# Padded on-chip pools and earlier first weight pieces in a two-layer hybrid trunk on one Trainium2 core

## The chip, the cores and the metric

The kernel runs on one core of one Trainium2 chip. The metric is the time of one execution on the device in microseconds; lower is better. Five engines of the core matter here: TensorE (PE) multiplies matrices, VectorE (DVE) and ScalarE (ACT) work element by element, GpSimd (POOL) does little, and SyncE (SP) issues nearly all DMA transfers. Each engine works through its own queue in order; semaphores make an engine wait for the result of another. SBUF is the on-chip memory that holds all operands, PSUM the one that receives products.

## The reference

Two layers, each a mixer and an MLP, on a residual stream of 512 tokens by 1024 features, all in float32:

```python
def rms_norm(x, gain):
    return x * rsqrt(mean(x * x, axis=-1) + 1e-6) * gain

# layer 0: mixer = multi-head latent attention (MLA), 8 heads
# layer 1: mixer = gated linear attention (GLA), 4 heads, chunks of 64
for i in range(2):
    xn = rms_norm(x, norm_mix[i])
    x = x + mixer_i(xn)                       # ends in "... @ w_o", 1024 x 1024
    xn = rms_norm(x, norm_mlp[i])
    hid = square(relu(xn @ w_up[i]))          # 1024 -> 4096
    x = x + hid @ w_down[i]                   # 4096 -> 1024
return rms_norm(x, final_norm)
```

GLA begins with `h = xn @ w_in`, whose columns are queries (512), keys (512), values (1024), gates (1024) and a low-rank forget gate (16). So the order of stages is: MLA, its output projection, MLP 0, GLA, its output projection, MLP 1, final norm.

## The kernel before

**Products.** Features lie on the 128 partitions, tokens along the rows: the stream is eight tiles `xT` of 128 by 512. To get float32 accuracy each operand is split into a rounded high part and a low part, and each product is three matmuls that add into one PSUM bank (`mm3`):

```python
    PE.matmul(psum, wh, xh, start=start, stop=False, **kw)   # L108
    PE.matmul(psum, wh, xl, start=False, stop=False, **kw)   # L109
    PE.matmul(psum, wl, xh, start=False, stop=stop, **kw)    # L110
```

A weight comes by DMA as `raw` or `wraw` and is split by `piece`: ACT rounds it into `wh` (L100), DVE subtracts into `wl` (L103); there are three buffers of each. So ACT and DVE make the weights that PE eats, one piece of 128 by 1024 for 24 matmuls of 256 columns or 12 to 24 of other widths.

**Output projection.** `out_proj` has four steps, c = 0 to 3. Each loads and splits 256 weight columns, multiplies two tiles (24 matmuls of 512 columns each), adds them to `xT` (DVE, L771), and hands each tile to the next norm: `add` starts the tile's square and its split into `x0h`, `x0l` to `x7h`, `x7l`, and `pair` builds the token-half combinations `T0` to `T3`.

**MLP.** The up product goes in blocks of 512 hidden columns; each block is cut in halves both ways, and seven products of quarters replace eight (steps `s1` to `s7`; "a11", "a12", "a21", "a22" are quarters of the weight, "11", "21", "22", "T1" to "T4" the combinations of x that meet them). The down product is arranged the same way. The last two blocks of the down product are plain: `down` makes eight tiles of 512 columns, adds them to `xT` (L1008) and hands them to the next norm, whose `add` is an ACT rounding (`set`, L232), an ACT square (`mt`), a DVE subtraction (`set`, L233) and a DVE sum (`acc`, L225).

**Where an MLP starts.** `mlp` is called after `out_proj`. It closes the pools `ps` and `stage`, opens `mps`, `down` and `down_w`, issues one 512-column matmul on the norm's last tile (`nrm.any`, L1056), and begins block 0 with `s1` (`unit`, a DMA of 512 KB; `piece`; 24 matmuls). Then `begin` finishes the norm: a mean over partitions by matmul (L242), then the reciprocal root on ACT and DVE (L119, L205 to L208).

**What sets the order.** The program is written without an order between engines; a scheduler puts each engine's instructions into its queue, by due time as it sees it, and buffers that come free. Pools are placed one after the other in SBUF, so the size of one sets the addresses of the next. The stationary operand of a matmul is the first after `psum` in the lines above, the moving one the second.

Of the kernel before, what the change touches and what calls it, by code (L numbers as in the profile page):

```python
# [18 lines left out]
P = 128  # L19
D = 1024  # L20
S = 512
# [28 lines left out]
def trunk_kernel(ctx: ExitStack, tc: tile.TileContext, t_in: dict, out: bass.AP, out_row: bass.AP):  # L50
# [93 lines left out]
    rk = rope_es.enter_context(tc.tile_pool(name="rope_keep", bufs=1, reuse_waits="tile"))  # L144
    gains = const.tile([P, N_GAIN], F32, name="gains")
    pos_i = rk.tile([P, NT], I32, name="pos_i")
    invf = rk.tile([P, 32], F32, name="invf")


# [98 lines left out]
    class QuadNorm(Norm):  # L248
# [7 lines left out]
        def scaled(self, j, src):  # L256
            pool = pool_of("up")
            lead = j < KH
            n = TH if lead else S
            hi, lo = (pool.tile([P, n], F32R, tag=f"x{j}{x}", name=uname(f"x{j}{x}")) for x in "hl")  # L260
            g = gcol(self.g, self.g0 + j)
            ACT.activation(hi, src[:, :n], AF.Copy, scale=g)
            DVE.scalar_tensor_tensor(lo, src[:, :n], g, f(hi), ALU.mult, ALU.subtract)
            if lead:
                self.quad["11"][j] = hi, lo
            else:
                self.any = hi
                for name, tk in (("21", first), ("22", second)):
                    self.quad[name][j - KH] = cut((hi, lo), slice(None), tk)

        def pair(self, k):
            pool = pool_of("up")
            g1, g2 = (gcol(self.g, self.g0 + j) for j in (k, k + KH))
            u, v = xT[k], xT[k + KH]
            t = pool.tile([P, 4, TH], F32, tag="raw", bufs=5, name=uname("pair"))
            t1, t2, t3, t4 = (t[:, i] for i in range(4))
            ACT.activation(t3, u[:, second], AF.Copy, scale=g1)
            DVE.scalar_tensor_tensor(t3, v[:, second], g2, t3, ALU.mult, ALU.subtract)
            DVE.scalar_tensor_tensor(t2, u[:, first], g1, t3, ALU.mult, ALU.add)
            DVE.scalar_tensor_tensor(t4, v[:, first], g2, t2, ALU.mult, ALU.subtract)  # L280
# [109 lines left out]
    def mla(layer, nrm, first, pools):  # L390
# [87 lines left out]
        for t in range(NT):  # L478
            tk = slice(t * P, (t + 1) * P)
            for hf in range(2):  # L480
                p = bank("bc"[hf])
                for k in range(2):
                    mm3(p, cut(CVL[k], slice(None), tk), cut(wv[k], slice(None), 0, slice(hf * 512, hf * 512 + 512)), k == 0, k == 1)
                if t == 0 and hf == 1:
                    pr = bank("b")
                    for i in range(NT):
                        tr(pr[:, i * 3 * RB : (i + 1) * 3 * RB], rows[:, i * P : (i + 1) * P])
                    cols = keep.tile([P, NT, 3], F32, tag="cols", name="cols")
# [267 lines left out]
        mms(range(n))  # L756
        return ps_, lambda: mms(range(n, ND))

    def out_proj(w2d, X, nxt, begun=None):
        for c in range(4):  # L760
            if c == 0:
                ps_, rest = begun or out_start(w2d, X, 0)
                rest()
            else:
                w = out_cols(w2d, c)
                ps_ = [bank("ac"[c % 2]), bank("ac"[c % 2])]
                for j in range(2):
                    a_type(ps_[j], w[j], X)
# [7 lines left out]
    def mlp(layer, nrm, nxt, final=False):  # L776
        w_up, w_dn = t_in["mlp_w_up"][layer], t_in["mlp_w_down"][layer]
        quad = nrm.quad
        NB = FF // FB
        closed("ps")  # L780
        opened("mps", space=bass.MemoryType.PSUM)
        closed("stage")
        dp, up, mp = opened("down"), pool_of("up"), pool_of("mps")
        wp = opened("down_w")

        def wide_raw():
            return wp.tile([P, 4, 512], F32, tag="raw", bufs=3, name=uname("raw"))

        def matmuls(p, w, k0, ks, ms, x, begin, end):
            for k in ks:  # L790
# [11 lines left out]

        def up_block(b):
            fh, s = b % 2, b // 2
            q = [dp.tile([P, 4, TH], F32, tag="q", bufs=6, name=uname("q")) for _ in range(2)]
            Q[s, fh] = q

            def unit(half, trail):
                if b == 1 and half == 0:
# [9 lines left out]
                return t  # L819

            def product(p, a, name, begin):
                w = piece(a, KH, 256)
                for j in range(2):
                    matmuls(p, w, 0, range(KH), [j], quad[name], begin, True)

# [7 lines left out]
                return t.rearrange("p (j t) -> p j t", j=2)  # L833

            def mt():
                return dp.tile([P, 512], F32, tag="mt", bufs=4, name=uname("mt"))

            v = {}

            def s1():  # L840
                a = v["a11"] = unit(0, 0)
                if b != 1:
                    v["a21"], v["a22"] = unit(1, 0), unit(1, 1)
                v["x1"] = bank("u")
# [5 lines left out]
                    seed(v["x1"])  # L850

            def seed(src):
                v["b2"] = mp.tile([P, 512], F32, tag="seed", name=uname("ps"))
# [46 lines left out]
            return [s1, s2, s5, s6, s3, s7, s4] if b < 2 else [s1, s5, s2, s6, s3, s7, s4]  # L900

        acc = {n: dp.tile([P, 4, TH], F32, tag=f"sum{n}", name=f"sum{n}_{layer}") for n in (1, 6, 7)}
        for n, (m0, tk) in {2: (0, first), 3: (0, second), 4: (KH, first), 5: (KH, second)}.items():
            acc[n] = xall[:, m0 : m0 + KH, tk]

        def down_block(s):
            last = s == NB // 2 - 2
# [78 lines left out]
            return [p1, p5, p6, p7, p2, p3, p4]  # L986

        def hidden(b, pool):
            hi, lo = (pool.tile([P, 4, S], F32R, tag="h" if pool is dp else "h" + x, bufs=2 if pool is dp else 1, name=uname("h" + x)) for x in "hl")
# [60 lines left out]
        def begin():  # L1050
            nrm.finish()
            for k in range(KH):
                DVE.tensor_tensor(xT[k][:, second], xT[k][:, second], xT[k + KH][:, second], ALU.subtract)

        t = mp.tile([P, 512], F32, tag="seed", name=uname("ps"))
        PE.matmul(t, nrm.any[:, :P], nrm.any, start=True, stop=True)  # L1056
# [19 lines left out]
        opened("ps", space=bass.MemoryType.PSUM)  # L1076
        hid = hidden(NB - 2, hp)
        down(NB - 2, hid)
        hid = hidden(NB - 1, dp)
        if final:  # L1080
            down_final(NB - 1, hid)
        else:
# [404 lines left out]
        opened("up", "right")  # L1487
        return QuadNorm(ND, inv_d, "mlp", g0, None)

    n_mlp0 = mlp_norm(0)  # L1490
    out_proj(t_in["mla_w_o"][0], O, n_mlp0, begun)

    class Mixer(Norm):
        def open(self):
            pool = opened("masks", "right")
            self.ident_i = pool.tile([P, P], I32, name="ident_i")
            DVE.tensor_copy(self.ident_i, ident)
            self.masks = {}
            for m in (1, 2, 4, 8):
# [9 lines left out]
    mlp(0, n_mlp0, n_mix1)  # L1509
    opened("stage")  # L1510
    Y = gla(0, n_mix1, "B", "B")
    closed("masks")
    n_mlp1 = mlp_norm(ND)
    out_proj(t_in["gla_w_o"][0], Y, n_mlp1)

    class Final:
        def open(self):
# [65 lines left out]
    mlp(1, n_mlp1, Final(), True)  # L1583
    for name in ("fin", "wide", "ps"):
        closed(name)


# [49 lines left out]
```

## Time and profile before

| | |
|---|---|
| median of 3 runs | 1122.13 us (1121.31 to 1123.38) |
| the profiled execution | 1124.27 us, of which the span is 1122.6 us |
| granted TensorE clock, mean | 0.983 |
| instructions | 17825 |
| MLA with its output projection | 0 to 196 us |
| MLP 0 | 196 to 532 us |
| GLA with its output projection | 532 to 777 us |
| MLP 1 and final norm | 777 to 1122.6 us |

Times inside the execution are counted from the start of the span. Where a row of the timeline reads "start us, us, engine line op out<-in", the second number is the instruction's own duration; consecutive matmuls overlap, so that the distance of two starts is what one costs. A number in square brackets at the end is how long the engine stood idle before that instruction, and what ended it. A row by windows gives, for each stretch, its length, then for PE, weight load, DVE, ACT and POOL the busy time with the count of instructions, then the granted clock and the share and rate of the DMA engines.

### The profile page before, as it was taken

Reading aid. Unit: us, or ns where it says so; the run is one execution under the profiler, and the core shown is the slowest. Engines: PE = TensorE matmul, PEld = TensorE weight load, DVE = VectorE, ACT = ScalarE, POOL = GpSimd, SP = SyncE. Lnnn points to the kernel's source line nnn. Section 1 sums busy time; section 2 is a strip of 40 time slices with the busy share of each in tenths; the row PEclk is TensorE's granted clock in tenths of the full one; section 3 lists DMA queues with packets and bytes.
Section 4 is the critical chain, followed back from the end, with each engine's and each line's share of the span. In section 5 each row is a group of like instructions: output and inputs, shape, how many; then the busy total and the mean of one; then the engine's idle time right before and its main releaser. Section 6 shows DMA issues by size and latency. Waiting matters only on the chain.

```text
span 1122.6 us, 17825 instructions
## 1 busy us (share of the span) xinstructions
PE 1087.1 (97%) x7320; PEld 994.2 (89%) x7320; DVE 892.7 (80%) x1210; ACT 641.0 (57%) x934; POOL 42.8 (4%) x78
## 2 busy tenths in 40 slices
PE   8999999889999999999799999999999999999997
PEld 6788887889999999987688888887989999999986
DVE  5789877889899899966365664667989899799865
ACT  5577654555666767653333743653556666776634
POOL 6300000000000000030000000000000000000000
PEclk9999999899999999999799999999999999999999
DMA  6412142133333423250232212431233523423312
GB/s 190 103 47 76 34 149 81 48 104 113 117 111 113 150 95 95 81 183 1 58 102 75 76 39 76 145 118 38 76 94 95 172 93 97 167 78 111 113 56 76
DMA packets 98001, 107.88 MB, mean 96 GB/s; under 512 B 8080, under 2 KB 72864, under 8 KB 97920
## 3 DMA queue, kind: packets, MB, share of 16 engines
q1 hardware_dynamic: 95904, 105.52, 29.9%
q10 hardware_dynamic: 1952, 1.21, 0.4%
q8 instruction: 57, 0.93, 0.3%
q0 software_dynamic: 64, 0.02, 0.1%
q14 instruction: 24, 0.20, 0.1%
HBM read 104.64 MB, written 2.10 MB: 95 GB/s over the span
## 4 chain that ended last, share of the span: by engine, by line
PE 87%; DVE 7%; ACT 2%; DMA 2%; issue 1%; SPq 0%; DVEq 0%; ACTq 0%
PE ps L108 27%; PE ps L110 27%; PE ps L109 26%; DVE wl L103 2%; PE ps L125 2%; PE ps L1301 2%; DMA wraw_ckv<-in_mla_w_in_dram 1%; ACT wh L100 1%; DMA raw<-in_mlp_w_up_dram 1%; DVE set L233 1%; DVE raw L877 1%; PE ps L656 0%; PE ps L1338 0%; PE ps L657 0%; PE ps L655 0%
## 5 line engine op out<-in xcount | busy, mean ns | idle before, releaser
L100 ACT ACTIVATE wh<-raw 128x1024 fp32r<-128x1024 f32 x208 | 219.8, 1059 | 183.4 <-PE ps L109 148.5
L103 DVE TENSOR_TENSOR wl<-raw,wh 128x1024 fp32r<-128x1024 f32 x208 | 252.6, 1224 | 22.5 <-ACT wh L100 21.8
L110 PE MATMUL ps<-h,wl 128*128 128x256 f32 x672 | 188.2, 280 | 2.8 <-DVE wl L103 2.7
L109 PE MATMUL ps<-h,wh 128*128 128x256 f32 x672 | 187.8, 280 | 0.0
L108 PE MATMUL ps<-h,wh 128*128 128x256 f32 x672 | 187.8, 279 | 0.0
L110 PEld LDWEIGHTS ps<-h,wl 128*128 128x128 f32 x672 | 126.4, 188 | 3.6 <-DVE wl L103 3.6
L109 PEld LDWEIGHTS ps<-h,wh 128*128 128x128 f32 x672 | 126.3, 188 | 0.0
L108 PEld LDWEIGHTS ps<-h,wh 128*128 128x128 f32 x672 | 126.3, 188 | 0.0
L108 PE MATMUL ps<-set,wh 128*128 128x512 f32 x232 | 93.5, 404 | 2.5 <-ACT set L232 2.5
L100 ACT ACTIVATE wh<-wraw 128x1024 fp32r<-128x1024 f32 x43 | 44.8, 1054 | 87.3 <-PE ps L110 42.4
L109 PE MATMUL ps<-set,wh 128*128 128x512 f32 x232 | 93.4, 403 | 1.0 <-DVE set L233 0.9
L110 PE MATMUL ps<-set,wl 128*128 128x512 f32 x232 | 92.8, 400 | 0.0
L103 DVE TENSOR_TENSOR wl<-wraw,wh 128x1024 fp32r<-128x1024 f32 x43 | 52.4, 1222 | 11.1 <-ACT wh L100 11.0
L103 DVE TENSOR_TENSOR h<-q,h 128x1024 fp32r<-128x1024 f32 x42 | 51.5, 1225 | 11.3 <-ACT h L100 11.3
L108 PE MATMUL ps<-wh,set 128*128 128x512 f32 x144 | 60.0, 417 | 0.0
L109 PE MATMUL ps<-wl,set 128*128 128x512 f32 x144 | 57.0, 396 | 0.0
L110 PE MATMUL ps<-wh,set 128*128 128x512 f32 x144 | 56.9, 395 | 0.0
L108 PEld LDWEIGHTS ps<-set,wh 128*128 128x128 f32 x232 | 44.5, 192 | 13.1 <-ACT set L232 3.1
L830 ACT ACTIVATE q<-q 128x512 f32<-128x512 f32 x64 | 40.0, 625 | 27.3 <-DVE q L829 26.9
L109 PEld LDWEIGHTS ps<-set,wh 128*128 128x128 f32 x232 | 44.5, 192 | 11.6 <-DVE set L233 1.7
L110 PEld LDWEIGHTS ps<-set,wl 128*128 128x128 f32 x232 | 44.6, 192 | 10.3
L100 ACT ACTIVATE h<-q 128x1024 fp32r<-128x1024 f32 x42 | 44.0, 1048 | 0.6 <-DVE q L964 0.6
(490 smaller groups left out, 3024.5 us busy)
## 6 DMA issues: line engine op xcount, KB each, us to landing
raw<-in_mlp_w_down_dram SPq DMA_DIRECT2D x38, 1024.0 KB, 5.3
raw<-in_mlp_w_up_dram SPq DMA_DIRECT2D x60, 512.0 KB, 3.8
wraw<-in_gla_w_in_dram SPq DMA_DIRECT2D x12, 1024.0 KB, 5.2
wraw<-in_mla_w_o_dram SPq DMA_DIRECT2D x8, 512.0 KB, 4.8
wraw<-in_gla_w_o_dram SPq DMA_DIRECT2D x8, 512.0 KB, 5.0
raw<-in_mlp_w_up_dram SPq DMA_DIRECT2D x2, 1024.0 KB, 6.6
xT<-in_x_dram SPq DMA_DIRECT2D x6, 256.0 KB, 8.3
wraw_qn<-in_mla_w_uq_dram SPq DMA_DIRECT2D x6, 256.0 KB, 3.4
```

Of the source, the lines that this page charges most:

```text
L100: order(ACT.activation(hi, src, AF.Copy))
L103: lo_eng.tensor_tensor(lo, src, f(hi), ALU.subtract)
L108: PE.matmul(psum, wh, xh, start=start, stop=False, **kw)
L109: PE.matmul(psum, wh, xl, start=False, stop=False, **kw)
L110: PE.matmul(psum, wl, xh, start=False, stop=stop, **kw)
L125: PE.transpose(psum, src, ident[: src.shape[0], : src.shape[0]])
L233: DVE.scalar_tensor_tensor(lo, src, g, f(hi), ALU.mult, ALU.subtract)
L830: ACT.activation(qs, qs, AF.Square)
L877: DVE.tensor_tensor(v["s"], v["s"], v["a11"], ALU.subtract)
L1301: PE.matmul(p[:, t * 64 : (t + 1) * 64].rearrange("p (n c) -> p n c", c=m), k[:, sl], later, start=True, stop=True)
```

## The change

**Pads.** Five pools get a dead first tile: `stage` 224 bytes per partition, a new pool `edge` on the right side 64, `up` 448, `masks` 256 and `rope_keep` 128 (`cols` moves into that pool). Read from the addresses of the two built programs: of 1664 matmuls with 512 columns, both operands now start at the same offset modulo 512 bytes, namely 416. Before, the pair (moving, stationary) was (480, 416) for 480 of them, (192, 416) for 480 and (416, 480) for 384; in the rest it was 0, 64 or 224 against 416, or 416 or 480 against 192. The 256-column matmuls stay as they were, nearly all at (480, 416) or (192, 416).

**First pieces of the MLPs.** `mlp` becomes a generator. `out_proj` runs it up to its first `yield` just after loading the weights of its last step, c = 3: a new step `s0` loads quarters a11 and a12 of block 0 and splits both. The pools are switched after that. Block 0 adds a21 + a22 in place and loads a22 once more for its last product (one more 512 KB transfer in each MLP). The matmul on `nrm.any` becomes two of 256 columns on `x0h`.

**First pieces of GLA.** In the last weight piece of MLP 0's `down`, `nxt.prefetch` loads the first 256 columns of GLA's `w_in` (1 MB) and splits two pieces into `self.qk`. No line of the program reads `self.qk`; `gla` loads and splits the same columns as before. The hidden tiles of MLP 0's last block move to the pool of those of the block before.

```diff
+    PADS = dict(stage=224, right=64, up=448, masks=256, keep=128)
+    def pad(pool, n):
+        if n:
+            pool.tile([P, n // 4], F32, tag="pad", name=uname("pad"))
...
-    opened("stage")
+    opened_stage()
+    pad(opened("edge", "right"), PADS["right"])
...
-    def out_proj(w2d, X, nxt, begun=None):
+    def out_proj(w2d, X, nxt, after, begun=None):
...
                 w = out_cols(w2d, c)
+                if c == 3:
+                    next(after)
...
-                w = piece(a, KH, 256)
+                w = v.pop(name) if name in v else piece(a, KH, 256)
...
+            def s0():
+                v["a11"], v["a12"] = unit(0, 0), unit(0, 1)
+                for name, a in (("11", v["a11"]), ("21", v["a12"])):
+                    v[name] = piece(a, KH, 256)
...
-                s = v["s"] = up.tile([P, KH, 256], F32, tag="raw", bufs=5, name=uname("raw"))
+                if b == 0:
+                    s = v["s"] = v["a22"]
+                else:
+                    s = v["s"] = up.tile([P, KH, 256], F32, tag="raw", bufs=5, name=uname("raw"))
...
             def s4():
+                if b == 0:
+                    v["a22"] = unit(1, 1)
...
+                    if b == NB - 1 and c == g == 1:
+                        nxt.prefetch(wide_raw())
...
-        PE.matmul(t, nrm.any[:, :P], nrm.any, start=True, stop=True)
-        blocks = [up_block(b) for b in range(NB)]
+        for h in range(2):
+            x = quad["11"][0][0]
+            PE.matmul(t[:, h * TH : (h + 1) * TH], x[:, :P], x, start=h == 0, stop=True, skip_group_check=True)
...
+        def prefetch(self, raw):
+            raw = raw.rearrange("p a (b n) -> p (a b) n", b=2)
+            SP.dma_start(raw, t_in["gla_w_in"][0][:, :256].rearrange("(k p) n -> p k n", p=P))
+            self.qk = [piece(raw[:, :, j * P : (j + 1) * P], ND, P) for j in range(2)]
```

Three places of the queues follow. Line numbers of the changed program are about ten higher in the helpers (L110 for L100, L113 for L103), and buffer numbers differ.

The first place is the end of MLA's output projection, on DVE, from the split of its last-but-one pair of tiles to the reciprocal root of the norm; `wl` rows are weight pieces. Before:

```order
L771 TENSOR_TENSOR xT<-ps_2136,xT 128x512
L278 SCALAR_TENSOR_TENSOR pair_2201<-xT,gains,pair_2201 128x256
L1053 TENSOR_TENSOR xT<-xT 128x256
L279 SCALAR_TENSOR_TENSOR pair_2201<-xT,gains,pair_2201 128x256
L103 TENSOR_TENSOR wl_2251<-raw_2243,wh_2250 128x1024
L263 SCALAR_TENSOR_TENSOR x7l_2195<-xT,gains,x7h_2194 128x512
L225 TENSOR_TENSOR acc_1930<-acc_1930,tmp_2198 128x512
L280 SCALAR_TENSOR_TENSOR pair_2201<-xT,gains,pair_2201 128x256
L281 SCALAR_TENSOR_TENSOR pair_2201<-xT,gains,pair_2201 128x256
L103 TENSOR_TENSOR T3l_2208<-pair_2201,T3h_2207 128x1024
L862 TENSOR_TENSOR raw_2391<-raw_2245,raw_2247 128x1024
L103 TENSOR_TENSOR wl_2299<-raw_2296,wh_2298 128x1024
```

After the change, from the last sum of a tile on:

```order
L274 SCALAR_TENSOR_TENSOR x7l_2213<-xT,gains,x7h_2212 128x512
L236 TENSOR_TENSOR acc_1936<-acc_1936,tmp_2216 128x512
L289 SCALAR_TENSOR_TENSOR raw_2219<-xT,gains,raw_2219 128x256
L884 TENSOR_TENSOR raw_2251<-raw_2249,raw_2251 128x1024
L290 SCALAR_TENSOR_TENSOR raw_2219<-xT,gains,raw_2219 128x256
L291 SCALAR_TENSOR_TENSOR raw_2219<-xT,gains,raw_2219 128x256
L912 TENSOR_TENSOR raw_2249<-raw_2141,raw_2249 128x1024
L113 TENSOR_TENSOR T3l_2226<-raw_2219,T3h_2225 128x1024
L216 SCALAR_TENSOR_TENSOR mt_2287<-ps_2280,mt_2285 128x512
L218 SCALAR_TENSOR_TENSOR mt_2289<-mt_2287,mt_2285 128x512
L113 TENSOR_TENSOR wl_2328<-raw_2324,wh_2327 128x1024
```

The two pieces of quarters a11 and a12 (`wl_2251`, `wl_2299` before) are gone from this stretch; they now stand ahead of the split of the last pair of tiles, and the first weight piece behind the last tile's sum is `wl_2328`, that of block 1.

The second place is ACT some 40 us further on, around the copies that seed the second block's products (L866 and L854 before, L888 and L873 after). Before:

```order
L100 ACTIVATE wh_2620<-raw_2328 128x1024
L100 ACTIVATE wh_2652<-raw_2549 128x1024
L830 ACTIVATE q_2227<-q_2227 128x512
L866 ACTIVATE mt_2584<-ps_2555 128x512
L854 ACTIVATE ps_2586<-mt_2359 128x512
```

After:

```order
L110 ACTIVATE wh_2617<-raw_2324 128x1024
L841 ACTIVATE q_2247<-q_2247 128x512
L888 ACTIVATE mt_2581<-ps_2552 128x512
L873 ACTIVATE ps_2583<-mt_2355 128x512
L110 ACTIVATE wh_2649<-raw_2546 128x1024
```

One rounding of a weight piece moved from ahead of the two copies to behind them.

The third place is the end of MLP 0, on DVE, in the last tiles of `down`; `raw_5768` is the load of `prefetch`:

```order
L236 TENSOR_TENSOR acc_5647<-acc_5647,mt_5692 128x512
L1035 TENSOR_TENSOR xT<-ps_5695,xT 128x512
L113 TENSOR_TENSOR wl_5771<-raw_5768,wh_5770 128x1024
L244 SCALAR_TENSOR_TENSOR set_5710<-xT,gains,set_5709 128x512
L236 TENSOR_TENSOR acc_5647<-acc_5647,mt_5713 128x512
L1035 TENSOR_TENSOR xT<-ps_5722,xT 128x512
L113 TENSOR_TENSOR wl_5775<-raw_5768,wh_5774 128x1024
L244 SCALAR_TENSOR_TENSOR set_5737<-xT,gains,set_5736 128x512
```

The two `wl` rows are new; before, the rows around them followed each other without them. On SP the new load stands ahead of GLA's own first load, which brings the same columns:

```order
L1021 DMA raw_5716<-in_mlp_w_down_dram 128x4x512
L1549 DMA raw_5768<-in_gla_w_in_dram 128x8x256
L140 DMA wraw_5830<-in_gla_w_in_dram 128x8x256
L140 DMA wraw_5906<-in_gla_w_in_dram 128x8x256
L140 DMA wraw_6058<-in_gla_w_in_dram 128x4x512
```

More of the change, by code (lines that the diff above doesn't have):

```diff
@@ L274, in pair @@
             u, v = xT[k], xT[k + KH]
-            t = pool.tile([P, 4, TH], F32, tag="raw", bufs=5, name=uname("pair"))
+            t = pool.tile([P, 4, TH], F32, tag="raw", bufs=5, name=uname("raw"))
             t1, t2, t3, t4 = (t[:, i] for i in range(4))
@@ L804, in up_block, with outputs @@
             fh, s = b % 2, b // 2
-            q = [dp.tile([P, 4, TH], F32, tag="q", bufs=6, name=uname("q")) for _ in range(2)]
-            Q[s, fh] = q
+            q = []
+            def outputs():
+                q.extend(pool_of("down").tile([P, 4, TH], F32, tag="q", bufs=6, name=uname("q")) for _ in range(2))
+                Q[s, fh] = q
             def unit(half, trail):
@@ L852, in seed @@
             def seed(src):
-                v["b2"] = mp.tile([P, 512], F32, tag="seed", name=uname("ps"))
+                v["b2"] = pool_of("mps").tile([P, 512], F32, tag="seed", name=uname("ps"))
                 ACT.activation(v["b2"], src, AF.Copy)
@@ L896, in s4 @@
             def s4():
+                if b == 0:
+                    v["a22"] = unit(1, 1)
                 product(v["b2"], v["a22"], "T4", False)
                 finish(pairs(v["b2"]), 1, first)
[L900 to L904, printed above, removed]
+            if b == 0:
+                return [s0, s1, s2, s5, s6, s3, s7, s4]
+            return [s1, s2, s5, s6, s3, s7, s4] if b == 1 else [s1, s5, s2, s6, s3, s7, s4]
         def down_block(s):
@@ L988, in hidden @@
         def hidden(b, pool):
-            hi, lo = (pool.tile([P, 4, S], F32R, tag="h" if pool is dp else "h" + x, bufs=2 if pool is dp else 1, name=uname("h" + x)) for x in "hl")
+            n = 1 if pool is not dp and final else 2
+            hi, lo = (
+                pool.tile([P, 4, S], F32R, tag="h" if pool is dp else "h" + x, bufs=n, name=uname("h" + x)) for x in "hl"
+            )
             for q, tk in zip(Q[b // 2, b % 2], (first, second)):
@@ L1053, in begin @@
                 DVE.tensor_tensor(xT[k][:, second], xT[k][:, second], xT[k + KH][:, second], ALU.subtract)
+        blocks = [up_block(b) for b in range(NB)]
+        blocks[0].pop(0)()
+        yield
+        pad(up, PADS["up"])
+        closed("ps")
+        mp = opened("mps", space=bass.MemoryType.PSUM)
+        closed("stage")
+        dp = opened("down")
+        opened("down_w")
+        acc = {n: dp.tile([P, 4, TH], F32, tag=f"sum{n}", name=f"sum{n}_{layer}") for n in (1, 6, 7)}
+        for n, (m0, tk) in {2: (0, first), 3: (0, second), 4: (KH, first), 5: (KH, second)}.items():
+            acc[n] = xall[:, m0 : m0 + KH, tk]
         t = mp.tile([P, 512], F32, tag="seed", name=uname("ps"))
-        PE.matmul(t, nrm.any[:, :P], nrm.any, start=True, stop=True)
-        blocks = [up_block(b) for b in range(NB)]
+        for h in range(2):
+            x = quad["11"][0][0]
+            PE.matmul(t[:, h * TH : (h + 1) * TH], x[:, :P], x, start=h == 0, stop=True, skip_group_check=True)
         lead = [blocks[b].pop(0) for b in (0, 0, 1, 1)]
@@ L1581, in row @@
                 q.dma_start(o[:, cs], y[:, cs])
-    mlp(1, n_mlp1, Final(), True)
-    for name in ("fin", "wide", "ps"):
+    mlp1 = mlp(1, n_mlp1, Final(), True)
+    out_proj(t_in["gla_w_o"][0], Y, n_mlp1, mlp1)
+    next(mlp1, None)
+    for name in ("fin", "wide", "ps", "edge"):
         closed(name)
```

34 lines of the change are left out of this document (18 added, 16 removed).

## The prediction

> **What bounds the kernel now.** I read the page first, then the chain of waits, then the span by windows, then the timelines of the starts of the MLPs.
>
> ```profile
> span 1122.6 us, 17825 instructions
> PE 1087.1 (97%) x7320; PEld 994.2 (89%) x7320; DVE 892.7 (80%) x1210; ACT 641.0 (57%) x934; POOL 42.8 (4%) x78
> PE 87%; DVE 7%; ACT 2%; DMA 2%; issue 1%; SPq 0%; DVEq 0%; ACTq 0%
> ```
>
> PE is busy for 97% and is 87% of the chain. So a change can help in three ways only: fewer gaps, a full clock, or a smaller distance between matmuls. Where the gaps are, the windows say (length, then PE, weight load, DVE, ACT, POOL busy, then clock):
>
> ```profile
> 195.60:253.20 57.60, 50.51 (x367) 48.09 (x366) 49.20 (x54) 29.89 (x39) 0.00 (x0) 0.91 0.24 74
> 237.50:241.00 3.50, 3.50 (x19) 3.50 (x18) 2.45 (x2) 0.34 (x1) 0.00 (x0) 0.51 0.96 347
> 253.20:480.00 226.80, 225.57 (x1926) 225.14 (x1926) 212.46 (x191) 148.52 (x168) 0.00 (x0) 1.00 0.35 112
> 777.40:836.00 58.60, 51.41 (x389) 49.05 (x388) 51.75 (x56) 31.50 (x40) 0.00 (x0) 0.94 0.25 73
> ```
>
> The first 58 us of each MLP hold 7.1 and 7.2 us of idle PE, and some stretches at half the granted clock; the 227 us behind the first of them hold 1.2. The changed starts aim at the right stretch. But DVE is busy for 49.2 and 51.8 us of these 58 too, so it stands close behind as the next bound.
>
> **First pieces of the MLPs.** These PE rows are the start of MLP 0, except the last, the same matmul of MLP 1 as the one at 210.98:
>
> ```profile
> 197.37 0.50 PE L1056 MATMUL ps<-x7h 128*128 128x512 f32 x1 [1.31 <-ACT x7h L262]
> 199.07 0.39 PE L110 MATMUL ps<-x0h,wl 128*128 128x256 f32 x1 [1.20 <-DVE wl L103]
> 205.00 0.39 PE L108 MATMUL ps<-x4h,wh 128*128 128x256 f32 x1 [0.66 <-ACT wh L100]
> 206.52 0.39 PE L108 MATMUL ps<-x0h,wh 128*128 128x256 f32 x1 [1.02 <-ACT wh L100]
> 210.98 0.28 PE L110 MATMUL ps<-x0h,wl 128*128 128x256 f32 x1
> 234.06 0.28 PE L110 MATMUL ps<-T3h,wl 128*128 128x256 f32 x1
> 236.43 0.39 PE L108 MATMUL ps<-x4h,wh 128*128 128x256 f32 x1 [2.09 <-ACT mt L866]
> 791.01 0.28 PE L110 MATMUL ps<-x0h,wl 128*128 128x256 f32 x1
> ```
>
> The first two waits (the matmul on the last tile, and `wl`) and the next two (`wh`) go, since both pieces are split before the tiles are done. What is late next is DVE. It runs this chain behind the last tile's sum; its durations, and the distance of two instructions in a row:
>
> ```profile
> 195.87 0.69 DVE L771 TENSOR_TENSOR xT<-ps,xT 128x512 f32<-128x512 f32 x1 [2.26 <-PE ps L110]
> 196.67 0.48 DVE L278 SCALAR_TENSOR_TENSOR pair<-xT,gains,pair 128x256 f32<-128x256 f32 x1
> 197.07 0.42 DVE L1053 TENSOR_TENSOR xT<-xT 128x256 f32<-128x256 f32 x1
> 198.93 0.75 DVE L263 SCALAR_TENSOR_TENSOR x7l<-xT,gains,x7h 128x512 fp32r<-128x512 f32 x1
> 199.60 0.69 DVE L225 TENSOR_TENSOR acc<-acc,tmp 128x512 f32<-128x512 f32 x1
> 200.20 0.48 DVE L280 SCALAR_TENSOR_TENSOR pair<-xT,gains,pair 128x256 f32<-128x256 f32 x1
> 215.03 1.22 DVE L890 TENSOR_TENSOR raw<-raw,raw 128x1024 f32<-128x1024 f32 x1
> 216.16 1.22 DVE L883 TENSOR_TENSOR raw<-raw,raw 128x1024 f32<-128x1024 f32 x1
> 777.51 0.69 DVE L771 TENSOR_TENSOR xT<-ps,xT 128x512 f32<-128x512 f32 x1 [2.26 <-PE ps L110]
> ```
>
> From start to start a 256-column instruction costs 0.40, a 512-column one 0.60 to 0.67, a 128x1024 one 1.13, and the sum of a tile, with what waits for it, 0.80. By the first place of the order, behind the sum at 195.87 come: two at 256 columns (0.73), `x7l` 0.67, `acc` 0.60, one at 256 (0.39), a weight sum 1.13, two at 256 (0.87), a weight difference 1.13, `T3l` 1.13 (a rounding of that size takes ACT 1.04, a row below shows, and hides behind that difference), two of the root at 0.60, and `wl_2328` 1.13. With 0.80 that is 9.8, and 0.1 more since the last counts to its end: 9.9 us. PE has 2 + 24 + 24 matmuls at 0.117 us (225.57 us over 1926 in the third window) and the mean over partitions to do meanwhile, some 7 us, so it then waits 2.9 us for `wl_2328`. That matmul came 15.1 us behind the sum before (195.87 to 210.98), and in MLP 1 13.5 (777.51 to 791.01). Gain to this point 5.2 and 3.6.
>
> Such a wait has a price behind it. The gap of 2.37 us at 234.06 is followed by the half-clock window from 237.5, where 19 matmuls take 3.5 us instead of 2.2. I charge the new wait one such window, 1.3 lost in each MLP. [...]
>
> Further on, the gap at 234.06 is PE waiting for the copy `mt` L866, which stands behind a rounding on ACT (1.04 long, some 0.96 from start to start); by the second place of the order that rounding now comes behind the copies. I take 0.96 off the gap, leaving 1.4, and with it its half-clock window, 1.3: no gap as short stands alone ahead of such a window. The other waits (0.4 at 228, 0.7 at 246.7) I leave. Sum: MLP 0 5.2 − 1.3 + 0.96 + 1.3 = 6.2; MLP 1, whose copies wait alike, 3.6 − 1.3 + 0.96 + 1.3 = 4.5; together **−10.7**. DVE could go along with that: its idle in these windows is 8.4 and 6.85, and two subtractions (2.26) leave each. The lead should last, since behind 253 DVE has 14 us of slack. Bounds: no gain beyond the first point and both prices paid, −6.2; no window and no later wait, −8.8 − 2 × (0.4 + 2.4 + 1.3 + 0.7) = −18.4, which the idle time of DVE just allows.
>
> **First pieces of GLA.** These don't do what they say: the pieces are made and not read, and GLA's own load and split stay. What is added is one 1 MB load, two roundings and two subtractions. The rows of the last tiles and of GLA's start:
>
> ```profile
> 516.67 1.22 DVE L103 TENSOR_TENSOR wl<-raw,wh 128x1024 fp32r<-128x1024 f32 x1 [0.23 <-ACT wh L100]
> 520.55 0.75 DVE L233 SCALAR_TENSOR_TENSOR set<-xT,gains,set 128x512 fp32r<-128x512 f32 x1 [0.79 <-ACT set L232]
> 523.30 0.75 DVE L233 SCALAR_TENSOR_TENSOR set<-xT,gains,set 128x512 fp32r<-128x512 f32 x1 [0.79 <-ACT set L232]
> 535.79 2.04 PE L242 MATMUL ps<-acc,inv 128*128 128x512 f32 x2 [3.28 <-DVE acc L225]
> 539.12 1.04 ACT L100 ACTIVATE wh<-wraw 128x1024 fp32r<-128x1024 f32 x1
> 543.23 0.80 PE L108 MATMUL ps<-set,wh 128*128 128x512 f32 x1
> wraw<-in_gla_w_in_dram SPq DMA_DIRECT2D x2, 1024.0 KB, 8.9
> ```
>
> In each tile DVE idles 0.79 of 2.75 us, waiting for ACT. Two subtractions of 1.22 fit two such holes but for 2 × 0.43, so the last `acc`, the mean and all behind it come 0.9 later; ACT's two roundings lie in its own idle time. The load goes ahead of GLA's own two on SP, but those, issued ahead of 500, take 8.9 us and are done 30 us before the rounding at 539.12 uses them. **+0.9** (0, if the tail's slack takes it, to +2.4, if none of it hides). The gap from 532 to 543 stays.
>
> **Pads.** A change of the distance between 512-column matmuls counts 1664 times. Rows from which it comes: first and last starts of 98 in a row with (moving, stationary) at (224, 416) with the last but one, of 93 at (192, 416), then a score product at (64, 64) and the one behind it, and the first and last of 37 with 256 columns at (192, 192):
>
> ```profile
> 487.98 0.40 PE L108 MATMUL ps<-hh,wh 128*128 128x512 f32 x1
> 509.97 0.39 PE L108 MATMUL ps<-hh,wh 128*128 128x512 f32 x1
> 510.19 0.39 PE L109 MATMUL ps<-hl,wh 128*128 128x512 f32 x1
> ...
> 510.65 0.40 PE L108 MATMUL ps<-hh,wh 128*128 128x512 f32 x1
> 532.12 0.39 PE L110 MATMUL ps<-hh,wl 128*128 128x512 f32 x1
> ...
> 149.93 0.39 PE L653 MATMUL ps<-kh,qh 128*128 128x512 f32 x1
> 150.16 0.39 PE L654 MATMUL ps<-kl,qh 128*128 128x512 f32 x1
> ...
> 725.92 0.28 PE L110 MATMUL ps<-set,AOl 128*128 128x256 f32 x1
> 730.24 0.28 PE L110 MATMUL ps<-set,ADl 128*128 128x256 f32 x1
> ```
>
> That is 229.0, 233.4 and, over eight such, 231.0 ns; over all 1664 the mean is 232.4, and the smallest distance that recurs is 226.5 (the last two of the first row). So addresses do bear on the distance, by some 2%, but alike ones hardly occur. For 256 columns they are against the change: 120.0 ns at (192, 192), 117 to 118 at the usual pairs. Bounds: 226.5 throughout, −9.8; the 120.0 doubled, 240.0, +12.6. I take the nearest row, 231.0: 1664 × 1.4 ns = **−2.3**. [...]
>
> **The sum.** −10.7 + 0.9 − 2.3 = −12.1. On the profiled execution: span 1122.6 to 1110.5, with the 1.7 us around it 1112.2. That execution (1124.27) lies 2.1 above the median 1122.13, so the forecast against the median is **1110 us**. The one more 512 KB load per MLP costs nothing: the DMA engines are busy for a quarter there.
>
> **The rivals.**
>
> The clock holds through the new wait. The two starts hold the same idle time (7.1 and 7.2), and yet the clock was 0.91 in the one and 0.94 in the other, so a low window depends on where a wait falls. Then 2.6 less: 1107.4. Against it: the 2.37 us gap above was paid for.
>
> Alike operands run at the floor of 226.5: for it, that such a distance occurs at all; against it, no long row has it. −9.8 for −2.3: 1102.5.
>
> Addresses do nothing, the rows differ for another reason: 1112.3.
>
> DVE keeps the lead. PE starts earlier but then waits for weights, and what it wins is what leaves DVE, two subtractions of 1.13 in each MLP, 4.5: 1116.2. For it: DVE is busy for 212 of the 227 us behind 253, too. Against: its 8.4 idle us before that, much of it waits that earlier matmuls shorten.
>
> Slower: alike operands lock at a bad distance, as the 256-column row at 120.0 does. At 240.0 the pads cost 12.6 and outweigh the −9.8 of the rest: 1124.9. It decides from 238.3 ns on (232.4 + 9.8 us / 1664). Against it: 231.0 at (64, 64), with the same 512 columns.
>
> **How the numbers follow.** Forecast 0.40, clock holds 0.13, floor 0.15, addresses nothing 0.15, DVE keeps the lead 0.09, slower 0.08. The range, 1101 to 1119, leaves out the slower case (0.08), the far part of the one in which DVE keeps the lead (0.03), and the floor joined with a clock that holds (0.06). A measurement of this kernel tells about 0.2%, 2.2 us. The slower case and a mishap of the same sign, in which the start gains its lower bound and the pads cost, give slower 0.08; what falls between it and a lead wholly kept by DVE, same 0.05, taken from that case and from the forecast's edge; the rest, faster 0.87.
>
> **What would show it.** In the profile after: no wait of PE on the first two weight pieces of each MLP, and one of about 2.9 us on `wl` some 7 us behind the last matmul of the output projection, with a half-clock window behind it; the mean of GLA 0.9 later against the last matmul of MLP 0; 512-column rows in a row at about 231 ns, at one distance in all stages. I am wrong if the distance is at either bound, or if PE waits again on `wl` in the 60 us behind the start for as long as it gained.

## The result and the profile after

The changed kernel takes 1105.13 us (median of 4 runs, 1103.56 to 1105.17) where the kernel before took 1121.72 (1121.25 to 1123.38): ratio 0.9846, interval 0.9829 to 0.9863, 16.6 us less. The forecast was 1110 in a range of 1101 to 1119.

The page of the kernel after, its span, busy times and chain of waits:

```profile
span 1103.5 us, 17836 instructions
PE 1071.4 (97%) x7322; PEld 985.7 (89%) x7322; DVE 895.1 (81%) x1212; ACT 643.1 (58%) x936; POOL 44.5 (4%) x78
PE 85%; DVE 10%; ACT 2%; issue 1%; DMA 0%; ACTq 0%; DVEq 0%
```

PE lost 16 us of busy time and the same share stays; in the chain DVE grew from 7% to 10%. Where the 19.1 us between the two profiled spans went is seen when both are cut at the same matmuls. This table is made from the starts of the first and last matmul of each stage in the timelines; "start" of an MLP runs from the last matmul of the output projection to the end of the first 48 matmuls of its down product.

| stage, us | before | after | difference |
|---|---|---|---|
| first 136 matmuls of MLA | 42.6 | 39.5 | −3.1 |
| rest of MLA and its output projection | 152.8 | 150.7 | −2.1 |
| start of MLP 0 | 65.9 | 59.6 | −6.3 |
| rest of MLP 0, without its tail | 226.7 | 225.3 | −1.3 |
| tail of MLP 0 (its two plain blocks, 192 matmuls) | 44.1 | 43.3 | −0.8 |
| gap to GLA's first matmul | 11.1 | 12.1 | +1.0 |
| GLA and its output projection | 233.8 | 231.4 | −2.4 |
| start of MLP 1 | 64.3 | 60.0 | −4.3 |
| rest of MLP 1, tail and end | 281.2 | 281.4 | +0.2 |

The first row is hardly the change's (136 matmuls at 227 instead of 229 ns make 0.3 us of it): 1.8 us of the difference are time in which the first matmuls wait for the splits of their tiles (3.4 us before, 1.6 after), and the row lies between 39.5 and 41.8 in the other runs below; the profiled execution of before was 2.5 us above that kernel's median. The windows of both starts after (the columns as in the prediction), with the stretch of the first in which PE waited and the one behind it up to the tail:

```profile
190.40:249.90 59.50, 54.57 (x438) 52.64 (x437) 54.60 (x58) 33.20 (x42) 0.00 (x0) 0.97 0.42 136
200.00:205.00 5.00, 4.25 (x24) 4.07 (x24) 4.97 (x6) 1.17 (x3) 0.00 (x0) 0.71 0.84 301
249.90:475.10 225.20, 222.92 (x1923) 222.31 (x1922) 211.19 (x192) 151.40 (x171) 5.37 (x10) 1.00 0.36 117
762.20:822.10 59.90, 54.66 (x437) 52.64 (x437) 54.84 (x58) 33.10 (x42) 0.00 (x0) 0.97 0.41 134
```

PE's waits in that stretch, the same two waits in MLP 1, the DVE row that ended the second in MLP 0, and the tail and the mean ahead of GLA, from the timelines of after:

```profile
198.49 0.39 PE L118 MATMUL ps<-x0h,wh 128*128 128x256 f32 x1 [0.93 <-ACT wh L110]
200.75 0.39 PE L120 MATMUL ps<-x0h,wl 128*128 128x256 f32 x1 [1.75 <-DVE wl L113]
226.48 0.39 PE L118 MATMUL ps<-x4h,wh 128*128 128x256 f32 x1 [1.08 <-ACT mt L888]
770.26 0.39 PE L118 MATMUL ps<-x0h,wh 128*128 128x256 f32 x1 [1.03 <-ACT wh L110]
772.52 0.58 PE L120 MATMUL ps<-x0h,wl 128*128 128x256 f32 x1 [1.75 <-DVE wl L113]
...
199.47 1.22 DVE L113 TENSOR_TENSOR wl<-raw,wh 128x1024 fp32r<-128x1024 f32 x1
...
475.19 0.40 PE L118 MATMUL ps<-hh,wh 128*128 128x512 f32 x1
518.50 0.39 PE L120 MATMUL ps<-hh,wl 128*128 128x512 f32 x1
523.15 2.05 PE L253 MATMUL ps<-acc,inv 128*128 128x512 f32 x2 [4.25 <-DVE acc L236]
```

The first two pieces are waited for no more. The next, block 1's, is: 0.93 us for `wh` and 1.75 for `wl`, with two matmuls between them, and the clock is then 0.71 from 200 to 205 us. In MLP 1 the waits are 1.03 and 1.75 us, and the clock is 0.72 over the 5 us from 770 on. The copy at 226.48 is waited for 1.08 instead of 2.09 us, and no low clock follows it (1.00 from 226.5 to 232). The 192 matmuls of the tail stand 226.8 ns apart (43.31 us over 191), where they stood 229.0 and 233.4 apart before. The mean ahead of GLA comes 4.65 us behind the last matmul instead of 3.67.

### The profile page after: what moved, and what is told of

It is laid out like the page before. It is cut to its first block, busy times and chain, and to the rows that moved or that the text cites. A ratio compares the mean times of both kernels' runs of the same rounds, so it can differ in the third digit from the quotient of the medians.

```text
span 1103.5 us, 17836 instructions
## 1 busy us (share of the span) xinstructions
PE 1071.4 (97%) x7322; PEld 985.7 (89%) x7322; DVE 895.1 (81%) x1212; ACT 643.1 (58%) x936; POOL 44.5 (4%) x78
## 4 chain that ended last, share of the span: by engine, by line
PE 85%; DVE 10%; ACT 2%; issue 1%; DMA 0%; ACTq 0%; DVEq 0%
PE ps L118 26%; PE ps L120 26%; PE ps L119 26%; DVE wl L113 3%; PE ps L135 2%; PE ps L1342 2%; ACT wh L110 1%; DVE raw L1000 1%; DVE h L113 1%; DVE raw L884 1%; DVE set L244 1%; DVE acc L236 1%; PE ps L1379 0%; DVE raw L899 0%; PE ps L666 0%
## 5 line engine op out<-in xcount | busy, mean ns | idle before, releaser
L110 ACT ACTIVATE wh<-raw 128x1024 fp32r<-128x1024 f32 x210 | 221.4, 1058 | 180.5 <-PE ps L119 141.5
L113 DVE TENSOR_TENSOR wl<-raw,wh 128x1024 fp32r<-128x1024 f32 x210 | 255.5, 1224 | 25.4 <-ACT wh L110 24.9
L110 ACT ACTIVATE wh<-wraw 128x1024 fp32r<-128x1024 f32 x43 | 44.8, 1055 | 85.2 <-PE ps L120 41.5
L113 DVE TENSOR_TENSOR wl<-wraw,wh 128x1024 fp32r<-128x1024 f32 x43 | 52.6, 1229 | 10.8 <-ACT wh L110 10.6
L113 DVE TENSOR_TENSOR h<-q,h 128x1024 fp32r<-128x1024 f32 x42 | 51.4, 1224 | 7.9 <-ACT h L110 7.9
L118 PEld LDWEIGHTS ps<-set,wh 128*128 128x128 f32 x232 | 44.5, 192 | 10.7 <-ACT set L243 1.8
L110 ACT ACTIVATE h<-q 128x1024 fp32r<-128x1024 f32 x42 | 44.1, 1049 | 0.8 <-DVE q L986 0.8
```

Of the source, the lines that this page charges most:

```text
L110: order(ACT.activation(hi, src, AF.Copy))
L113: lo_eng.tensor_tensor(lo, src, f(hi), ALU.subtract)
```

## Experiments: one part at a time

Theory A: the starts gave 10.6 us (the expectation below has 10.8), GLA's start took 1.0, and the distance of the 512-column matmuls gave the rest, 4 ns each. Theory B: the pads also act on the 256-column matmuls, whose distance changed too, although their addresses did not.

**Pads alone**, in the kernel before.

```diff
-    opened("stage")
+    opened_stage()                      # pad 224
+    pad(opened("edge", "right"), 64)    # and up 448, masks 256, keep 128, as in the change
```

> The kernel before with the pads alone; the starts of the MLPs and of GLA as they were. 1568 of 1664 512-column products then have both operands at 416. Theory A (the pads act through the 512-column distance alone, 4.0 ns less as in the profile after, the starts did the rest): 1568 x 4.0 ns = 6.3 us less, 1115.4 us, the 256-column products at 117.8 ns as before. Theory B (the pads also bring the 256-column products to the smaller distance of 113.3 ns that the profile after shows in long stretches): up to 2600 x 4.4 ns more, 1104 to 1110 us. By the prediction's own price (1.4 ns): 1119.5.

Measured 1114.05 us, ratio 0.9944 (0.9923 to 0.9965): 6.4 us less than before. Theory A's size, and nearly three times the prediction's.

**Starts alone**: all pads zero.

```diff
-    PADS = dict(stage=224, right=64, up=448, masks=256, keep=128)
+    PADS = dict(stage=0, right=0, up=0, masks=0, keep=0)
```

> The changed kernel with all pads zero: early first pieces and the unread GLA pieces stay. Theory A: the starts gain 10.8 (6.4 and 4.4 up to the same matmul), GLA's start loses 1.0: 1111.9 us, 512-column distance 232.4 ns. Theory B (much of the gain is the pads'): 1115 to 1118 us.

Measured 1104.47 us, ratio 0.9859 (0.9839 to 0.9879). Both theories fall: without any pad the kernel is as fast as with all of them, and the starts alone give 16. The two parts don't add. Cut like the table above, the starts take 57.2 and 57.1 us here, against 59.6 and 60.0 with the pads, and all 512-column stages but the tail are as slow as before. So the pads gain 4.4 us in MLA, the tail, GLA and the two output projections, and cost 5.4 at two places. The window of MLP 0's start, and what SP issues there, in this kernel:

```profile
192.90:250.20 57.30, 53.75 (x439) 51.90 (x438) 54.22 (x59) 33.22 (x43) 0.00 (x0) 1.00 0.29 88
...
151.09 0.37 SPq L824 DMA_DIRECT2D raw<-in_mlp_w_up_dram  x1
151.50 1.13 SPq L934 DMA_DIRECT2D raw<-in_mlp_w_down_dram  x2
161.38 0.99 SPq L754 DMA_DIRECT2D wraw<-in_mla_w_o_dram  x2
162.42 48.45 SPq L829 DMA_DIRECT2D raw<-in_mlp_w_up_dram  x7
```

and in the full change:

```profile
160.92 26.82 SPq L829 DMA_DIRECT2D raw<-in_mlp_w_up_dram  x4
187.91 0.39 SPq L824 DMA_DIRECT2D raw<-in_mlp_w_up_dram  x1
```

L824 is the 1 MB load of block 1's weights. Without pads it is issued at 151, with them at 188, behind four loads of block 0, the last of which waits 10.4 us for a scratch buffer, until DVE is done with `T2l`, and goes out at 187.38. The addresses of the two built programs tell why: the pad of 224 bytes moves the end of the `stage` pool 224 bytes into the first buffer of `down_w`, which used to begin just behind it. With the load late, the order puts block 1's roundings and subtractions behind the whole chain that the prediction adds up; without the overlap `wl` of block 1 stands ahead of a weight sum (L884), `T3l` and a weight difference (L912), and the clock stays at 1.00. On DVE without pads:

```profile
196.33 1.22 DVE L113 TENSOR_TENSOR wl<-raw,wh 128x1024 fp32r<-128x1024 f32 x1
...
199.39 1.22 DVE L884 TENSOR_TENSOR raw<-raw,raw 128x1024 f32<-128x1024 f32 x1
200.52 1.22 DVE L113 TENSOR_TENSOR T3l<-raw,T3h 128x1024 fp32r<-128x1024 f32 x1
...
202.26 1.22 DVE L912 TENSOR_TENSOR raw<-raw,raw 128x1024 f32<-128x1024 f32 x1
```

**No unread GLA pieces.**

```diff
-                    if b == NB - 1 and c == g == 1:
-                        nxt.prefetch(wide_raw())
```

> The changed kernel without the unread load and pieces at the end of MLP 0. Theory A (DVE's two subtractions push the last sum and all of GLA back by 0.9 to 1.0): 1104.1 us, and 11.1 us instead of 12.1 between the last matmul of MLP 0 and GLA's first. Rival (the tail has slack, the 1.0 came from elsewhere): no difference, 1105.1.

Measured 1106.78 us, ratio 0.9877 (0.9857 to 0.9896), not faster than the full change. In the trace the mean's row, then DVE's sum of the last tile, here and in the kernel before (whose last matmul starts at 532.12):

```profile
520.41 0.39 PE L120 MATMUL ps<-hh,wl 128*128 128x512 f32 x1
524.56 2.05 PE L253 MATMUL ps<-acc,inv 128*128 128x512 f32 x2 [3.77 <-DVE acc L236]
...
521.59 0.68 DVE L1033 TENSOR_TENSOR xT<-ps,xT 128x512 f32<-128x512 f32 x1
...
532.81 0.69 DVE L1008 TENSOR_TENSOR xT<-ps,xT 128x512 f32<-128x512 f32 x1
```

The mean waits 3.77 us, between the 3.28 of before and the 4.25 of after. So the two subtractions cost 0.5, half of what I had put down to them; that is within what the medians can't tell. The other half stays without them, and it follows from the shorter distance: the sum starts 1.18 us behind the last matmul here, 0.69 before. A tile takes DVE 2.75 us. Before, its twelve matmuls took PE 2.80 us, so that DVE made up 0.05 per tile behind the last weight piece; now they take 2.72, and DVE falls back by 0.03. Over the six tiles behind that piece the difference is 0.5. The run of pads alone bears this out: its last block's matmuls still stand 233.4 ns apart, and its mean waits 3.28 us as before.

**GLA reads the pieces made ahead.**

```diff
         def proj_qk(c):
-            raw = col_chunk(w_in, c * 256, 256)
-            w = [piece(raw[:, :, j * P : (j + 1) * P], ND, P) for j in range(2)]
+            if c == 0:
+                w = nrm.qk
+            else:
+                raw = col_chunk(w_in, c * 256, 256)
+                w = [piece(raw[:, :, j * P : (j + 1) * P], ND, P) for j in range(2)]
```

> The changed kernel in which GLA's first product reads the two pieces made ahead and its own load and split of the same columns are dropped. GLA's first matmuls then wait only for the last split of x, not for the reciprocal root and the pieces behind it: the gap of 12.1 us shrinks to 4 to 6 and its half-clock stretch with it, 1096 to 1100 us. Rival (GLA's next pieces stand behind the same root on ACT and DVE, so the gap moves behind the first product): 1103 to 1105 us.

Measured 1093.46 us, ratio 0.9755 (0.9731 to 0.9778): 11.7 us below the full change, more than I expected. The last matmul of MLP 0 and the first of GLA:

```profile
522.14 0.39 PE L120 MATMUL ps<-hh,wl 128*128 128x512 f32 x1
522.36 0.39 PE L118 MATMUL ps<-set,wh 128*128 128x512 f32 x1
```

The gap of 12.1 us is gone whole (0.23 is the distance of two matmuls), and the stages of GLA behind it take what they took (190.5 us against 191.4), so nothing of it came back.

## Experiments: the overlap of two pools

Theory C: the pads' cost is the late load that comes from the 224 bytes of overlap. Theory D: the parts fail to add because of the 256-column distance.

**The overlap without new offsets**: one pad of 512 bytes, so that all addresses keep their place modulo 512.

```diff
-    PADS = dict(stage=224, right=64, up=448, masks=256, keep=128)
+    PADS = dict(stage=512, right=0, up=0, masks=0, keep=0)
```

> The changed kernel with one pad only, 512 bytes ahead of the stage pool: every operand keeps the offset modulo 512 that it has without pads, but the stage pool now ends 512 bytes inside the first weight buffer of the MLP, so that block 1's first load is issued behind the four loads of block 0. Theory C (in the full change the pads gain some 5.3 us in the 512-column products and lose as much again at both MLP starts, because that load and with it block 1's pieces come late): 1104.5 + 5.4 = 1109.9 us, starts of 59.6 and 60.0 us instead of 57.2 and 57.1. Theory D (pads and starts fail to add for another reason, the lock of the 256-column products): 1104.5 us, no change.

Measured 1111.44 us, ratio 0.9924 (0.9899 to 0.9949): 7.0 us above the version without pads, 1.5 more than theory C had. The starts take 59.8 and 61.1 us, and the 512-column stages what they take without pads (37.1 for the output projection of MLA, 41.2 for GLA's). The load is issued late again:

```profile
162.52 27.47 SPq L829 DMA_DIRECT2D raw<-in_mlp_w_up_dram  x4
190.16 0.39 SPq L824 DMA_DIRECT2D raw<-in_mlp_w_up_dram  x1
```

The run of pads alone has the overlap too. The load in the kernel before, and with pads alone:

```profile
151.90 0.37 SPq L813 DMA_DIRECT2D raw<-in_mlp_w_up_dram  x1
...
187.11 0.39 SPq L825 DMA_DIRECT2D raw<-in_mlp_w_up_dram  x1
```

Yet the starts take 64.0 and 65.6 us there, together about what they took before (65.9 and 64.3). So the late load costs time only where the first pieces are early, and that is most of why the parts don't add.

**All pads without the overlap**: a spacer ahead of the weight buffers.

```diff
+        pad(opened("gap"), PADS["stage"])
         opened("down_w")
...
         closed("down_w")
+        closed("gap")
```

> The changed kernel with all its pads, and a spacer pool of 224 bytes ahead of the MLP's weight buffers, so that none of these overlaps the stage pool and block 1's load is issued early again. Theory C: both gains together, 1105.1 - 5.4 = 1099.7 us. Theory D: 1105 us.

Measured 1099.30 us, ratio 0.9813 (0.9787 to 0.9839). Theory C's number is met within 0.4 us. Start of MLP 0, the stretch that had the low clock, and the load:

```profile
190.40:247.50 57.10, 53.87 (x439) 52.01 (x438) 53.92 (x58) 33.27 (x42) 0.00 (x0) 1.00 0.29 87
200.00:205.00 5.00, 4.49 (x38) 4.28 (x37) 5.00 (x6) 1.01 (x2) 0.00 (x0) 1.00 0.35 105
149.71 0.37 SPq L824 DMA_DIRECT2D raw<-in_mlp_w_up_dram  x1
```

Starts of 57.0 and 57.1 us, as without pads, and the 512-column stages as with them. Against before that is 20.5 us, still less than the 22.4 of the two parts alone: in the profiles both parts shorten the rest of MLP 0 (by 1.8 and 1.6 us, and together by 1.2), and the gap to GLA is 10.2 and 11.5 us in the parts, 12.1 here.

**Both**: the spacer, and GLA reads its pieces.

> The same spacer, and GLA's first product reads the pieces made ahead. If the two gains add: 1093.5 - 5.4 = 1088.1 us. If one takes from the other: 1091 to 1094 us.

Measured 1087.98 us (1087.8 to 1088.83), ratio 0.9711 (0.9686 to 0.9735). The gains add, and this version beats the full change by 17 us.

## Experiments: what an address does

**Matmuls alone.** Series of 48, with the moving operand 0 to 480 bytes behind the stationary one, modulo 512.

> Not the trunk but matmuls alone (the output is zeros): series of 48 matmuls, 512 then 256 columns, where the moving operand's address stands 0, 32, 64, ... 480 bytes behind the stationary one modulo 512; at the end 256 columns at a difference of 64, four times with one to four small matmuls ahead. Theory E (the distance of two matmuls is set by the difference modulo 512): 512 columns about 227 at 0, 229 at 64, 233 at 288 (the difference of 192 against 416); 256 columns 120 at 0 and one value at 64 however the series begins. Theory F (the distance is a lock that depends on how the series begins): 256 columns at 64 take either 113.3 or 117.8 depending on what stands ahead.

The starts of four series of 512 columns in a row at 0, 32, 64 and 96 (the last only to end the third), then of those at 256, 288 and 320, from the timeline of that run:

```profile
33.97 0.74 PE L76 MATMUL p<-X,W 128*128 128x512 f32 x2 [0.69 <-ACT r L78]
45.89 0.73 PE L76 MATMUL p<-X,W 128*128 128x512 f32 x2 [0.75 <-ACT r L78]
58.10 0.50 PE L76 MATMUL p<-X,W 128*128 128x512 f32 x1 [0.75 <-ACT r L78]
70.11 0.50 PE L76 MATMUL p<-X,W 128*128 128x512 f32 x1 [0.75 <-ACT r L78]
...
131.16 0.50 PE L76 MATMUL p<-X,W 128*128 128x512 f32 x1 [0.75 <-ACT r L78]
143.10 0.73 PE L76 MATMUL p<-X,W 128*128 128x512 f32 x2 [0.75 <-ACT r L78]
155.31 0.50 PE L76 MATMUL p<-X,W 128*128 128x512 f32 x1 [0.75 <-ACT r L78]
```

A series takes 11.92, 12.21, 12.01 us at 0, 32, 64, and 11.94, 12.21 at 256 and 288: what counts is the difference modulo 256. Within a series, behind the first eight, the distances in ns are:

| difference modulo 256 | 0 | 32 | 64 | 96 | 128 | 160 | 192 | 224 |
|---|---|---|---|---|---|---|---|---|
| 512 columns | 226.7 | 233.3 | 228.9 | 233.3 | 232.2 | 234.3 | 233.3 | 233.3 |
| 256 columns | 120.0 | 117.8 | 117.8 | 120.1 | 118.6 | 117.3 | 117.8 | 118.4 |

This is theory E for 512 columns, with 256 in place of 512, and the table explains the two long rows of the prediction: (224, 416) differs by 64 modulo 256 (229.0), (192, 416) by 32 (233.4). It is the difference and not the moving address: the stationary operand stands at 128 modulo 512 in these series and at 416 in the trunk, and the pair (416, 480) of the kernel before, which differs by 192, stands at 233.2. For 256 columns alike is the worst but one, 120.0, as the rows at (192, 192) had it. No series at 64 ran at 113.3, whatever stood ahead of it.

**The same in the kernel, modulo 256.** The next three have the same instructions in the same order and differ in addresses alone.

> The version with the spacer once more, on the same chip as the next two, which have the same instructions in the same order and differ from it in addresses alone: 1099.3 us.

Measured 1100.24 us (1099.36 to 1101.35).

```diff
-    PADS = dict(stage=224, right=64, up=448, masks=256, keep=128)
+    PADS = dict(stage=480, right=64, up=448, masks=256, keep=128)
```

> The version with the spacer, and the stage pool pushed on by 256 more bytes: 604 of the 512-column products then differ by 256 modulo 512 instead of 0. If what counts is the difference modulo 256, as the series of matmuls alone have it (226.7 ns at 0, 226.8 at 256): 1099.3 us, no change, these products at 227 to 228 ns. If it is modulo 512, as the change's words have it: 604 x 5 to 6 ns = 3.0 to 3.6 us more, 1102.6 us.

Measured 1100.75 us (1099.26 to 1103.57): no change, and the products at (160, 416) stand 228.2 ns apart, those at (416, 416) 228.3. Modulo 256 it is.

```diff
-    PADS = dict(stage=224, right=64, up=448, masks=256, keep=128)
+    PADS = dict(stage=192, right=64, up=448, masks=256, keep=128)
```

> The version with the spacer, and the stage pool's pad 32 bytes smaller: 600 of the 512-column products then differ by 32 modulo 256. By the series of matmuls alone (233.3 ns at a difference of 32 or 224): 600 x 6.5 ns = 3.9 us more, 1103.2 us, these products at 233 ns. If the trunk's distance comes from something else that the pads moved: no change, 1099.3 us.

Measured 1103.28 us (1101.79 to 1104.63), 3.0 us above the version with the spacer; the products at (384, 416) stand 234.1 ns apart, the others 228.4. First and last of the same 160 rows in MLA's output projection, with the spacer (second run) and here:

```profile
154.65 0.45 PE L120 MATMUL ps<-set,wl 128*128 128x512 f32 x1
190.75 0.39 PE L120 MATMUL ps<-set,wl 128*128 128x512 f32 x1
...
155.56 0.45 PE L120 MATMUL ps<-set,wl 128*128 128x512 f32 x1
192.72 0.40 PE L120 MATMUL ps<-set,wl 128*128 128x512 f32 x1
```

From first to last that is 36.10 and 37.16 us. The stages that hold these products, MLA and GLA with their output projections, take 2.0 and 2.2 us more; the tail, whose addresses stay, takes 43.3 us in both. The address alone makes the difference.

**Two distances at one address.** In the trunk the 256-column matmuls at (480, 416), a difference of 64, keep to 117.8 ns over many series and to 113.3 over others, with the same addresses. Twenty-four of the same product before (first and last), and after:

```profile
289.60 0.28 PE L108 MATMUL ps<-T0h,wh 128*128 128x256 f32 x1
292.31 0.28 PE L110 MATMUL ps<-T3h,wl 128*128 128x256 f32 x1
```

```profile
237.23 0.28 PE L118 MATMUL ps<-T0h,wh 128*128 128x256 f32 x1
239.84 0.28 PE L120 MATMUL ps<-T3h,wl 128*128 128x256 f32 x1
```

That is 117.8 and 113.5. The trace of before has it only at 430 to 461, where a wait of 1.18 us follows, and in parts of MLP 1; the one after for most of MLP 0. Some of the changes from one to the other stand at waits of PE, others I could not tie to one. I tried to make it with a weight that comes late inside a series:

> Not the trunk but matmuls alone (the output is zeros): series of 72 matmuls of 256 columns at a difference of 64, 32 and 0 bytes, the seventeenth of which waits for a weight that ACT writes late, by 18 different delays; then 512 columns at 0. Theory F (a wait inside a series decides which of two distances it keeps): behind the wait some series at 64 run at 113.3 ns, others at 117.8, as the trunk has both with the same addresses. Theory G (the trunk's second distance needs more than a wait, such as the buffers around it): 117.8 in all of them, as without a wait.

The weight came too early: no series waited, so that the run doesn't tell F from G. At 64 all of them took 117.8. At 32 some took 117.8 and others 116.7, with the same addresses, so something other than the address decides between two distances there; where the 113.3 comes from stays open. It is worth little here: the rest of MLP 0 behind its start takes 226.6 us with 117.8 throughout (the version in which GLA reads its pieces) and 225.3 with 113.3 for most of it. I put this down to DVE, which is busy for 211 of these 225 us.

## Why the prediction was right, and where not

**Starts of the MLPs: right, in size and by its steps.** Forecast −6.2 and −4.5, measured −6.3 and −4.3. The one wait of 2.9 us came as 0.93 on `wh` and 1.75 on `wl`, and the low clock that I charged for it came too: 0.71 from 200 to 205 us behind 2.7 us of waiting with two matmuls in it, and 0.72 from 770 to 775 with 2.8 us of waiting in MLP 1. The copy further on was waited for 1.08 instead of 2.09, forecast 0.96 less, and without a low clock, as forecast. What the sum didn't show is why block 1's piece stood so late in the order: it took the order as given, and the order was the pads' doing. That step was right for this program and would have been wrong for the same change without pads.

**First pieces of GLA: right that they do nothing, and +1.0 for +0.9.** But the two subtractions are only half of that, so the size is luck: the other half is the shorter distance in the tail, which leaves DVE no time to catch up, and the sum had no term for it.

**Pads: the term was mis-sized**, −2.3 for −5.3 by the table (−2.1 and −0.8 in the two stages ahead of GLA, −2.4 in GLA and its projection), 6.4 in the run of pads alone. The step that failed is the choice of the nearest row, 231.0 at (64, 64). Those were score products, five matmuls on one bank, and they stand at 231 in the changed kernels too (231.1 with both operands at 160), for a reason that stays open; long series of alike operands run at 226.8. I had this as the rival that runs at the floor, chance 0.15, and its 1102.5 came nearer to 1105.1 than my 1110. The slower rival, the 120.0 of 256 columns doubled, was wrong because the difference 0, nearly the worst for 256 columns (120.0), is the best for 512 (226.7). The rival in which addresses do nothing falls by the run with the smaller stage pad: 234.1 against 228.4 ns with the same instructions in the same order. By what means an address slows a matmul no run shows.

**The sum** then lacks 4.5 us of the 16.6: 3.0 of the pads, and 1.1 by which the rest of both MLPs got shorter (−1.3, +0.2), the distance of 113.3 perhaps among it; the starts and GLA came 0.1 short each. The remaining 0.6 is less than the scatter. The price of the pads at the two starts (5.4) was inside the forecast's −10.7, and is what the full change lost.

## What to carry to other kernels

Size a pool and you also move every pool behind it (here 224 bytes ahead of `stage` put a load from 151 to 188 us): after a pad, compare when each load is issued, not only the offsets that the pad was for. A piece made ahead is worth its whole gap only where the consumer reads it, so look for the reader; here that alone was 11.7 us. In a chain like this, read the order of the changed program and add up the rows of what stands ahead of the late piece: that forecast both starts within 0.2 us.

## What the runs showed of the hardware

With a new weight for each, the distance of two fp32r matmuls of 512 columns goes from 226.7 to 234.3 ns with the difference of the two operands' addresses modulo 256 bytes, best at 0, then 64 (228.9), as series of matmuls alone have it; with 256 columns it is 117.3 to 120.1, and 0 is nearly the worst. At one and the same address a stream of 256 columns can keep to 113.3 or to 117.8 ns for hundreds of matmuls. A wait of PE of 2.7 us, with two matmuls in it, was followed by a clock of 0.71 from 200 to 205 us (the wait ends at 200.75). The sum of the waits alone doesn't decide it: before, waits of 0.66 and 1.02 us at the start of MLP 0 (205.00 and 206.52) were followed by a clock of 0.51 from 206.8 to 210.2, and waits of 0.77 and 1.02 us at the same place of MLP 1 were not (1.00 from 787.1 to 790.5).
